# A two-layer streaming encoder step: activations, memory, states and vectors handed over as columns, weights by granules

## The chip, the cores and the metric

The kernel runs on one core of one Trainium2 chip. The metric is device time in microseconds, the median of three runs. Beside it there is one profiled execution with a trace, from which all views below come.

## The reference

One inference step of a two-layer encoder over a prompt of 512 tokens and a sample of 32 tokens that carries state. Each sub-layer is followed by a LayerNorm of `ALPHA * x + sublayer(x)`. All data is float32, model width 1024.

```python
def run_trunk(x, pos, mem_k, mem_v, states, ...):
    for layer in range(DEPTH):                       # DEPTH = 2
        x = post_norm(x, 0.5 * swiglu(x, ffn_up[layer, 0], ffn_down[layer, 0]), ...)
        if layer % 2 == 0:
            y, st = mixer_ab(x, pos, *states[layer], ...)   # RG-LRU beside chunked retention
        else:
            y, st = mixer_c(x, *states[layer], ...)         # RWKV-7 time mixing
        x = post_norm(x, y, ...)
        x = post_norm(x, cross_attn(x, mem_k[layer], mem_v[layer], xa_q[layer], xa_o[layer]), ...)
        x = post_norm(x, 0.5 * swiglu(x, ffn_up[layer, 1], ffn_down[layer, 1]), ...)
    return x, new_states

def reference(x_prompt, x_sample, mem_prompt, state_conv0, ..., cache_mem_k, cache_mem_v, ...):
    mem_k_p = jnp.einsum('bmd,lde->lbme', mem_prompt, xa_k)   # 256 memory rows, 4 heads of 256
    mem_v_p = jnp.einsum('bmd,lde->lbme', mem_prompt, xa_v)
    y_prompt, st_p = run_trunk(x_prompt, pos_p, mem_k_p, mem_v_p, zero_states, ...)
    y_sample, st_s = run_trunk(x_sample, pos_s, cache_mem_k[..], cache_mem_v[..], sample_states, ...)
    return (y_prompt, y_sample, mem_k_p, mem_v_p, *st_p, *st_s)
```

The feed-forward is `(silu(x @ gate) * (x @ up)) @ down` with an inner width of 2816. RWKV-7 keeps a 64x64 state in each of 16 heads.

## The kernel before

**Layout.** Activations lie as columns: the model width on partitions (8 blocks of 128), tokens along the row. The 544 tokens are two halves: A has tokens 0 to 255, B has 256 to 511 and the 32 of the sample (288 in all). Each half has x (tiles XA, XB) and x split in two parts that matmuls take exactly, high (XHA, XHB) and low (XLA, XLB); HH and HL hold the same for a sub-layer's inner result.

**Weights.** A weight matrix is cut in granules of 1024 (or 896) rows by 128 columns, 512 KB. A granule is loaded by SyncE (SP) to one of three raw buffers `wr`, split by ACT (high part, line 486) and by DVE or GpSimd (low part, lines 408 and 412) to one of five slots `W`, and used by `linear`: for each of 8 blocks the high and the low weights with the high x, then the high weights with the low x, 24 matmuls into a PSUM bank `mm`. Mostly A and B share a granule; in and around layer 1's mixer each half loads its own stream (`SOLO`), so that A can run ahead.

**Order.** Each part is a Python generator. A planner (`Clock`) gives every instruction a start by its own costs and due times and hands that to the scheduler as a priority; the order on each engine, and which of DVE and GpSimd takes a low part (`ett`), come out of that. Each engine and each DMA queue works strictly in its own order. So a change in one part may move instructions far away.

**What comes in and goes out as rows.** x, the memory, the cached keys, the parameter vectors and the small states arrive as rows of tokens or of 128 numbers and are turned to columns by transposes on TensorE (`K.tr`, line 400, against the identity `identt`), through the PSUM banks `ax` or `mm`, and read from there by ACT and DVE. `load_x` does it for x at the start, half A ahead of B; `store_x` turns the result back at the end, again through `ax`, with copies to `arena` and stores by SP. `mem_kv` computes the memory's keys and values for both layers, 32 granules threaded into the first feed-forward: each key block is stored as it is to the scratch `kt`, transposed, and stored to the output; each value block is transposed, and stored to the output and to the scratch `vt`. `attend` transposes the cached keys of the sample.

**RWKV in layer 1.** Chunks of 32 tokens run one after another (`wkv_chain`), the state in two tiles Y in turn (one is tile Q, the other a raw buffer wr). Beside the chain, `wkv_solve` solves a triangular system for each block of tokens by rows on GpSimd: multiplications into P and subtractions in LC (line 412), with the system fetched from the scratch `dn` and the result passed through the scratch `dz` to W. The last block is the sample's: it begins with the sample's state, loaded as rows and transposed. `state_out` transposes the final states of the prompt (after block 7) and of the sample (after block 8) and stores them by GpSimd's queue.

Of the kernel before, what the change touches and what calls it, by code (L numbers as in the profile page):

```python
# [22 lines left out]
NT = NA + NB  # L23
# [350 lines left out]
class Kern(Clock):  # L374
# [228 lines left out]
    def _load(self, s):  # L603

        k, g = s["next_raw"], s["g"]
        if k >= s["limit"] or len(s["raw"]) >= NRAW - 1 or len(self.raws.free) <= self.kept[1]:
            return None
        self.raws.free.sort(key=lambda t: t[:2])
        if self.raws.free[0][0] > self.now:
            return self.raws.free[0][0]  # L610
        r = self.raws.pop()
        ap, kc, m = g[k][:3]
        self.end = self.now
        self.dma(r[:, :kc, :m], ap.rearrange("(c p) m -> p c m", p=128))
        s["raw"][k] = (r, self.end)
        s["next_raw"] += 1
        return self.now
# [84 lines left out]
def load_params(K):  # L702
# [19 lines left out]
    two.append(("shift1", i["state_shift1"].rearrange("b j (r p) -> (b j r) p", p=128), 8))
    groups.append(two)
    tot = sum(n for g in groups for _, _, n in g)
    K.pv = K.pool.tile([128, tot], F32, name="pv")
    col = 0
    for g in groups:
        blk = yield from K.ar.take((128,))
        st, = blk
        r = 0  # L730
        for n, ap, k in g:
            K.dma(st[r:r + k], ap)
            VEC[n] = col + r
            r += k
        ps = yield from K.aux.take()
        K.tr(ps[:, :r], st[:r])
        K.vcopy(K.pv[:, col:col + r], ps[:, :r])
        K.aux.give(ps)
        blk.free()
        col += r  # L740
# [22 lines left out]
def program(K):  # L763
# [98 lines left out]
def half_main(K, h):  # L862
# [20 lines left out]
    yield from store_x(K, h)  # L883
# [11 lines left out]
def load_x(K, h):  # L895
# [5 lines left out]
    st = K.slot("HH" + h.name, [128, 8 * n])  # L901
    parts = [(K.i["x_prompt"][0, h.c0 + t * 128:h.c0 + t * 128 + 128], t * 128, 128, st[:, t * 1024:t * 1024 + 1024])
             for t in range(2)]
    if h is K.B:
        parts.append((K.i["x_sample"][0], 256, 32, K.slot("HLB", [128, 8 * n])[:, :1024]))
    for src, t0, m, st in parts:
        K.dma(st[:m], src)
    K.go = True
    yield
    for src, t0, m, st in parts:  # L910
        for q in range(2):
            ps = yield from K.aux.take()
            p3 = ps.rearrange("p (a b) -> p a b", a=4)
            for c in range(4):
# [5 lines left out]
            K.aux.give(ps)  # L920
            yield
    event(K, "x", h.name).fire(K)
    yield K.done()


def store_x(K, h):
    parts = [(K.o["y_prompt"][0, h.c0 + t * 128:h.c0 + t * 128 + 128], t * 128, 128) for t in range(2)]
    if h is K.B:
        parts.append((K.o["y_sample"][0], 256, 32))
    blks = []  # L930
    for dst, t0, m in parts:
        blk = yield from K.ar.take((1024,))
        blks.append(blk)
    for q in range(2):
        for (dst, t0, m), blk in zip(parts, blks):
            st = blk.aps[0][:m, q * 512:q * 512 + 512]
            ps = yield from K.aux.take()
            for c in range(4):
                K.tr(ps[:m, c * 128:c * 128 + 128], h.x[:, q * 4 + c, t0:t0 + m])
            (K.vcopy if t0 == 128 else K.act)(st, ps[:m])  # L940
            K.aux.give(ps)
            K.dma(dst[:, q * 512:q * 512 + 512], st)
    yield
    yield K.done()
    for blk in blks:
        blk.free()


def store_states(K):

    for e in ("tail", "h"):
        for j in range(4):
            yield event(K, e, "B", j)
    yield event(K, "shift", "B")
    blk = yield from K.ar.take((128,))
    st, = blk
    ps = yield from K.aux.take()
    K.tr(ps[:48, :128], K.ov)
    K.vcopy(st[:48], ps[:48, :128])
    K.aux.give(ps)  # L960
    o = K.o
    yield K.done()
    for nm, a, r in (("p_conv", 0, 12), ("s_conv", 12, 12)):
        K.dma(o[nm].rearrange("b j (r p) -> (b j r) p", p=128), st[a:a + r])
    for nm, a, r in (("p_lru", 24, 4), ("s_lru", 28, 4)):
        K.dma(o[nm].rearrange("b (r p) -> (b r) p", p=128), st[a:a + r])
    for nm, a, r in (("p_shift", 32, 8), ("s_shift", 40, 8)):
        K.dma(o[nm].rearrange("b j (r p) -> (b j r) p", p=128), st[a:a + r])
    yield K.done()
    blk.free()  # L970
# [97 lines left out]
def post_ln(K, h, l, e, whole=False, final=False):  # L1068
# [53 lines left out]
def mem_kv(K):  # L1122
# [10 lines left out]
    for l in range(2):  # L1133
        for ap in (i["xa_k"][l], i["xa_v"][l]):
            for j in range(8):
                gran.append(ap[:, j * 128:j * 128 + 128])
# [7 lines left out]
    for t in range(2):  # L1144
        K.dma(st, i["mem_prompt"][0, t * 128:t * 128 + 128])
        p3 = ps.rearrange("p (a b) -> p a b", a=4)
        for q in range(2):
            for c in range(4):
                K.tr(p3[:, c], st[:, (q * 4 + c) * 128:(q * 4 + c) * 128 + 128])
            hi, lo = mh[:, q * 4:q * 4 + 4, t * 128:t * 128 + 128], ml[:, q * 4:q * 4 + 4, t * 128:t * 128 + 128]  # L1150
            K.act(hi, p3)
            K.tt(lo, p3, hi.bitcast(F32), ALU.subtract)
# [4 lines left out]
    for g, ap in enumerate(gran):  # L1157
# [3 lines left out]
        dst = K.o["mem_v" if kind else "mem_k"][l, 0].rearrange("(t p) h d -> p t (h d)", p=128)  # L1161
        yield K.ready([raw])
        K.dma(raw, ap.rearrange("(c p) m -> p c m", p=128))
# [73 lines left out]
def attend(K, h, l, hd, q, hh, hl, c0, m, qe, fin):  # L1237
# [11 lines left out]
    else:  # L1249
        K.dma(r3[:, 0], K.i["cache_mem_k"][l, 0, :, hd].rearrange("(c p) d -> p c d", p=128))  # L1250
# [3 lines left out]
    if c0 == 0:  # L1254
        K.act(ks[:, 0], raw[:, 0])
        K.tt(ks[:, 1], raw[:, 0], ks[:, 0].bitcast(F32), ALU.subtract)
    else:
        ps = yield from K.aux.take()
        p3 = ps.rearrange("p (c n) -> p c n", c=2)
        for a in range(2):  # L1260
            for b in range(2):
                K.tr(p3[:, b, a * 128:a * 128 + 128], r3[:, 0, a, b * 128:b * 128 + 128])
        K.act(ks[:, 0], ps)
        K.tt(ks[:, 1], ps, ks[:, 0].bitcast(F32), ALU.subtract)
        K.aux.give(ps)
# [317 lines left out]
def setup_mix1(K):  # L1583
# [7 lines left out]
    K.dma(K.w2a2[0:64], i["l1_w2"])  # L1591
    K.dma(K.w2a2[64:128], i["l1_a2"])
# [9 lines left out]
def lora_weights(K, h):  # L1602
# [10 lines left out]
    for t, u, nm, p in ((g1, gm, "l1_g1", 5), (wa[:, :, 0:64], wm[:, :, 0:64], "l1_w1", 3),  # L1613
                        (wa[:, :, 64:128], wm[:, :, 64:128], "l1_a1", 4)):
        yield K.ready([t])
        K.dma(t, K.i[nm].rearrange("(c p) m -> p c m", p=128))
# [319 lines left out]
def state_out(K, w, Y, dst):  # L1936
    blk = yield from K.ar.take((16, 64))
    st, = blk
    for q in range(2):
        ps = yield from w.pl.take()  # L1940
        for g in range(8):
            K.tr(ps[0:64, g * 64:g * 64 + 64], Y[0:64, 8 * q + g])
        K.act(st[0:64, 8 * q:8 * q + 8], ps[0:64].rearrange("p (g k) -> p g k", g=8))
        w.pl.give(ps)
# [137 lines left out]
```

## Time and profile before

| What | Value |
|---|---|
| median of three runs | 2989.22 us (2982.29 to 2990.96) |
| the profiled execution's own time | 2981.34 us |
| its span in the profile | 2979.5 us |
| mean granted TensorE clock | 0.952 |
| instructions on PE / DVE / ACT / GpSimd | 22456 / 3094 / 2182 / 1201 |
| bytes read from and written to HBM | 313.09 MB, 13.92 MB |
| packets of the SP queue | 603328, for 310.93 MB |

A row of the trace has the time from the span's start, how long the instructions took, engine, line, operation and `out<-in` by tile names without buffer numbers; in brackets the idle time of the engine just before and what ended it. PE is TensorE's matmuls, PEld its weight loads, POOL is GpSimd, SPq SyncE's issue of DMAs. The chain is the work that ended last, followed back from the end.

### The profile page before, as it was taken

The numbers are of one execution on the slowest core, as the hardware profiler recorded it, in microseconds if no ns is written. First come the engines' busy times: TensorE is split into PE (matmuls) and PEld (weight loads), VectorE is DVE, ScalarE is ACT, GpSimd is POOL, SyncE is SP. The second block draws the span as 40 slices with busy tenths as digits, with TensorE's granted clock in tenths as the row PEclk, the third lists the DMA queues.
The fourth block names the chain that finished last, engine by engine and source line by source line (L and its number), as shares of the span: only waits on it lengthen the run. The fifth ranks groups of instructions, "written<-read, shape, count | busy, mean of one in ns | idle before, by whom it ended". The sixth has DMA issues, their size and how long they took to land.

```text
span 2979.5 us, 54689 instructions
## 1 busy us (share of the span) xinstructions
PE 2809.6 (94%) x22456; PEld 2701.7 (91%) x22456; DVE 1765.9 (59%) x3094; ACT 1276.8 (43%) x2182; POOL 909.1 (31%) x1201
## 2 busy tenths in 40 slices
PE   8999998999998999998999899799779989999998
PEld 8999998898898999998999899578678878999997
DVE  5333436677767333356345655877588657765665
ACT  4323233665555222234234443444345454654444
POOL 2000104433314000023001212588577764241311
PEclk9999999999999999999999999799678889999999
DMA  6443443223232332322346554133122245546563
GB/s 184 124 120 116 134 117 107 77 75 90 89 98 71 100 89 82 93 79 85 86 138 184 143 145 128 38 90 98 42 70 80 75 115 167 149 144 181 167 174 94
DMA packets 611035, 330.56 MB, mean 111 GB/s; under 512 B 29032, under 2 KB 603840, under 8 KB 610784
## 3 DMA queue, kind: packets, MB, share of 16 engines
q1 hardware_dynamic: 603328, 310.93, 36.3%
q0 software_dynamic: 7456, 16.13, 2.0%
q8 instruction: 176, 2.88, 0.4%
q14 instruction: 75, 0.61, 0.1%
HBM read 313.09 MB, written 13.92 MB: 110 GB/s over the span
## 4 chain that ended last, share of the span: by engine, by line
PE 71%; DVE 11%; POOL 7%; ACT 5%; issue 3%; DMA 3%; SPq 0%; DVEq 0%; ACTq 0%; POOLq 0%
PE mm L395 65%; PE ax L395 5%; POOL LC L412 2%; POOL P L412 2%; DVE W L408 2%; ACT arena L486 2%; DVE arena L408 1%; DVE arena L432 1%; ACT W L486 1%; PE ax L400 1%; DVE XA L408 1%; DMA wr<-in_ffn_up 1%; POOL arena L412 1%; ACT L2043 1%; DVE XB L408 1%
## 5 line engine op out<-in xcount | busy, mean ns | idle before, releaser
L486 ACT ACTIVATE W<-wr 128x1024 fp32r<-128x1024 f32 (+1 forms) x558 | 577.7, 1038 | 725.8 <-PE mm L395 587.1
L408 DVE TENSOR_TENSOR W<-wr,W 128x1024 fp32r<-128x1024 f32 (+1 forms) x453 | 562.4, 1244 | 541.2 <-ACT W L486 536.8
L395 PE MATMUL mm<-XHB,W 128*128 128x288 f32 x3840 | 581.0, 300 | 15.4 <-ACT XHB L486 4.8
L395 PEld LDWEIGHTS mm<-XHB,W 128*128 128x128 f32 x3840 | 528.3, 190 | 24.1 <-ACT XHB L486 5.8
L395 PE MATMUL mm<-XHA,W 128*128 128x256 f32 x3840 | 530.8, 288 | 16.4 <-ACT XHA L486 6.6
L395 PEld LDWEIGHTS mm<-XHA,W 128*128 128x128 f32 x3840 | 494.8, 193 | 25.9 <-ACT XHA L486 10.8
L412 POOL TENSOR_TENSOR W<-wr,W 128x1024 fp32r<-128x1024 f32 (+1 forms) x105 | 253.9, 2419 | 659.7 <-ACT W L486 652.7
L395 PE MATMUL mm<-XLB,W 128*128 128x288 f32 x1984 | 313.6, 298 | 1.4 <-DVE XLB L408 1.4
L395 PE MATMUL mm<-HHB,W 128*128 128x288 f32 x1920 | 291.6, 302 | 9.7 <-ACT W L486 3.5
L395 PE MATMUL mm<-XLA,W 128*128 128x256 f32 x1984 | 290.5, 285 | 2.3 <-POOL XLA L412 2.3
L395 PE MATMUL mm<-HHA,W 128*128 128x256 f32 x1920 | 271.7, 290 | 14.5 <-DVE XA L408 5.0
L395 PEld LDWEIGHTS mm<-XLB,W 128*128 128x128 f32 x1984 | 281.2, 190 | 3.4 <-DVE XLB L408 1.9
L395 PEld LDWEIGHTS mm<-HHB,W 128*128 128x128 f32 x1920 | 268.7, 192 | 12.8 <-ACT W L486 4.5
L395 PEld LDWEIGHTS mm<-HHA,W 128*128 128x128 f32 x1920 | 250.7, 194 | 20.5 <-ACT W L486 5.3
L395 PEld LDWEIGHTS mm<-XLA,W 128*128 128x128 f32 x1984 | 261.6, 191 | 4.5 <-POOL XLA L412 2.5
L486 ACT ACTIVATE arena<-mm 128x256 f32<-128x256 f32 (+4 forms) x292 | 112.6, 388 | 308.2 <-PE mm L395 289.9
L432 DVE SCALAR_TENSOR_TENSOR arena<-mm,arena 128x288 f32<-128x288 f32 (+1 forms) x176 | 77.3, 439 | 161.7 <-PE mm L395 143.7
L395 PE MATMUL mm<-HLB,W 128*128 128x288 f32 x896 | 142.7, 299 | 0.0
L395 PE MATMUL mm<-HLA,W 128*128 128x256 f32 x896 | 129.9, 284 | 0.0
L412 POOL TENSOR_TENSOR SUMA<-XA 128x256 f32<-128x256 f32 x16 | 14.4, 901 | 377.3 <-DVE XA L408 360.7
L395 PEld LDWEIGHTS mm<-HLB,W 128*128 128x128 f32 x896 | 129.3, 192 | 0.1
L412 POOL TENSOR_TENSOR LC<-LC,P 128x66 f32<-128x66 f32 (+24 forms) x279 | 122.7, 440 | 20.6
(430 smaller groups left out, 3769.6 us busy)
## 6 DMA issues: line engine op xcount, KB each, us to landing
wr<-in_ffn_up SPq DMA_DIRECT2D x246, 512.0 KB
wr<-in_ffn_down SPq DMA_DIRECT2D x96, 448.0 KB
wr<-in_l_w_rkv SPq DMA_DIRECT2D x48, 512.0 KB
wr<-in_ffn_down SPq DMA_DIRECT2D x40, 512.0 KB
wr<-in_l_w_in SPq DMA_DIRECT2D x24, 512.0 KB
wr<-in_l_w_out SPq DMA_DIRECT2D x24, 512.0 KB
wr<-in_xa_q SPq DMA_DIRECT2D x24, 512.0 KB
wr<-in_xa_o SPq DMA_DIRECT2D x24, 512.0 KB
```

The lines of the kernel that those rows point to most:

```text
L395: self.nc.tensor.matmul(out, lhsT, rhs, start=start, stop=stop)
L400: self.nc.tensor.transpose(out, in_, self.ident[k0:k0 + k, k0:k0 + k])
L408: self.nc.vector.tensor_tensor(out, a, b, op=op)
L412: self.nc.gpsimd.tensor_tensor(out, a, b, op=op)
L432: self.nc.vector.scalar_tensor_tensor(out, a, s, b, op0=op0, op1=op1)
L486: return self.nc.scalar.activation(out, a, f, bias=bias, scale=scale, **kw)
L2043: nc.scalar.preload_act_table_set(name)
```

## The change

The host now hands the inputs over in the layouts in which the kernel keeps them (`lay`), and takes the outputs as columns (`unlay`). On the chip this removes the transposes of x, the memory, the cached keys, the vectors, the RWKV states and the outputs, and their reads from PSUM. Weights lie in HBM granule by granule, each as 128 rows of 4 KB (3.5 KB for 896 rows) in the place of 1024 pieces of 512 B. The values of the memory keep their transposes, since attention reads them as rows.

```diff
 _load:
-        self.dma(r[:, :kc, :m], ap.rearrange("(c p) m -> p c m", p=128))
+        self.dma(r[:, :kc, :m], ap)
 load_params (three groups of vectors, 20 loads and 3 transposes, become one load):
+    K.pv = K.pool.tile([128, i["pv"].shape[1]], F32, name="pv")
+    K.dma(K.pv, i["pv"])
 program:
-            gran.append((ap[k0:k1, m:m + 128], (k1 - k0) // 128, 128))
+            gran.append((ap[m // 128, :, k0 // 128:k1 // 128], (k1 - k0) // 128, 128))
 load_x:
-    for src, t0, m, st in parts:
-        K.dma(st[:m], src)
+    for c in range(0, 8, 2):
+        (K.dma, K.adma)[c // 2 % 2 if h is K.A else 0](h.x[:, c:c + 2], K.i["x"][:, c:c + 2, h.c0:h.c0 + n])
...
-                K.tr(p3[:, c, :m], st[:m, (q * 4 + c) * 128:(q * 4 + c) * 128 + 128])
-            d = (slice(None), slice(q * 4, q * 4 + 4), slice(t0, t0 + m))
-            K.act(h.xh[d], p3[:, :, :m])
-            K.tt(h.xl[d], p3[:, :, :m], h.xh[d].bitcast(F32), ALU.subtract)
-            K.vcopy(h.x[d], p3[:, :, :m])
+    for c in range(0, 8, 2):
+        u = slice(c, c + 2)
+        K.act(h.xh[:, u], h.x[:, u])
+        K.tt(h.xl[:, u], h.x[:, u], h.xh[:, u].bitcast(F32), ALU.subtract)
 store_x is gone; post_ln, last LayerNorm:
             first(c)
             second(c)
+            if final:
+                K.dma(K.o["y"][:, c, h.c0:h.c0 + n], x[:, c])
 store_states (a transpose and six stores become one store):
+    K.dma(K.o["ov"], K.ov)
 mem_kv:
+        K.gdma(K.o["mem_v" if kind else "mem_k"][l, j * 128:j * 128 + 128], a)
         if kind == 0:
             K.gdma(K.kt[l][j * 128:j * 128 + 128], a)
+            yield K.done()
+            continue
...
-        K.gdma(dst[:, :, j * 128:j * 128 + 128], b)
-        if kind:
-            K.gdma(K.vt[l].rearrange("(t p) d -> p t d", p=128)[:, :, j * 128:j * 128 + 128], b)
+        K.gdma(K.vt[l].rearrange("(t p) d -> p t d", p=128)[:, :, j * 128:j * 128 + 128], b)
 attend (sample half):
-        K.dma(r3[:, 0], K.i["cache_mem_k"][l, 0, :, hd].rearrange("(c p) d -> p c d", p=128))
+        K.dma(r3[:, 0], K.i["cache_k"][l, hd])
...
-                K.tr(p3[:, b, a * 128:a * 128 + 128], r3[:, 0, a, b * 128:b * 128 + 128])
-        K.act(ks[:, 0], ps)
+    K.act(ks[:, 0], raw[:, 0])
 wkv_chain (the sample's block, and the two final states):
-            K.dma(st[0:64], K.i["state_wkv1"][0].rearrange("h v k -> v h k"))
-            yield K.done()
-            for q in range(2):
-                for g in range(8):
-                    K.tr(b1[0:64, g * 64:g * 64 + 64], st[0:64, 8 * q + g])
-                K.act(Y[0:64, 8 * q:8 * q + 8], b1[0:64].rearrange("p (g k) -> p g k", g=8))
+            yield K.ready([Y[0:64]])
+            K.dma(Y[0:64], K.i["wkv0"])
...
-                yield from state_out(K, w, Yn, K.o["p_wkv"][0])
+                K.gdma(K.o["p_wkv"], Yn[0:64])
```

What this does to the order, at three places.

TensorE at the start. XHA, XLA and XHB are the parts of x, HHA and HHB hold its rows before, `mm` and `ax` are PSUM banks. Before:

```order
L400 MATMUL ax_67<-identt,HHA_93 128x128 x4
L395 MATMUL mm_63<-XHA_91,W_1_71 128x256
L400 MATMUL ax_68<-identt,HHB_101 128x128 x4
L400 MATMUL ax_69<-identt,HHB_101 128x128 x4
L395 MATMUL mm_64<-XHA_91,W_2_72 128x256
L395 MATMUL mm_63<-XHA_91,W_1_71 128x256 x15
L395 MATMUL mm_63<-XLA_92,W_1_71 128x256 x8
```

And now, from PE's first instruction on:

```order
L395 MATMUL mm_63<-XHA_91,W_1_71 128x256 x16
L395 MATMUL mm_63<-XLA_92,W_1_71 128x256 x8
L395 MATMUL mm_64<-XHA_91,W_2_72 128x256 x16
L395 MATMUL mm_64<-XLA_92,W_2_72 128x256 x8
L395 MATMUL mm_65<-XHB_100,W_1_71 128x288 x16
```

Half A's first two weight blocks no longer have the transposes of half B's rows among them; half B comes in third.

ACT at the end, from the LayerNorm of half B's last sub-layer on. Before, with the reads of the transposed result from `ax`:

```order
L486 ACTIVATE arena_79<-ax_70 128x288
L486 ACTIVATE arena_79<-arena_79,epst 128x288
L486 ACTIVATE arena_79<-arena_79 128x288
L486 ACTIVATE XB_98<-XB_98,pv,lng_345 128x288 x8
L486 ACTIVATE arena_79<-ax_69 128x512
L486 ACTIVATE arena_79<-ax_68 32x512
L486 ACTIVATE arena_79<-ax_67 128x512
L486 ACTIVATE arena_79<-ax_69 32x512
```

And now:

```order
L486 ACTIVATE arena_79<-XB_99 128x288 x8
L486 ACTIVATE arena_79<-ax_68 128x288
L486 ACTIVATE arena_79<-arena_79,epst 128x288
L486 ACTIVATE arena_79<-arena_79 128x288
L486 ACTIVATE XB_99<-XB_99,pv,lng_195 128x288 x8
```

The normalised columns are the engine's last work; SP's last rows are the eight stores of them.

GpSimd at the end of the last solve. P and LC are the solve's tiles, `dz` the scratch through which its result goes. Before:

```order
L412 TENSOR_TENSOR P_115_17677<-LC_7380,P_115_17677 128x16
L412 TENSOR_TENSOR LC_7380<-LC_7380,P_115_17677 128x8x2
L491 DMA out_p_wkv<-arena_80 64x16x64
L412 TENSOR_TENSOR P_115_17677<-LC_7380,P_115_17677 128x8
L412 TENSOR_TENSOR LC_7380<-LC_7380,P_115_17677 128x8
L491 DMA dz_17682<-LC_7380 128x1x32
```

And now:

```order
L412 TENSOR_TENSOR LC_7233<-LC_7233,P_112_17512 128x7x7
L412 TENSOR_TENSOR P_112_17512<-LC_7233,P_112_17512 128x42
L491 DMA out_p_wkv<-Q_113_17514 64x1024
L412 TENSOR_TENSOR LC_7233<-LC_7233,P_112_17512 128x7x6
L412 TENSOR_TENSOR P_112_17512<-LC_7233,P_112_17512 128x35
```

The store of the prompt's state stands ahead of the solve's last eleven instructions instead of its last two, and it goes directly from tile Q, into which SP then loads the sample's state (`in_wkv`); behind that load SP has weight loads of half A.

More of the change, by code (lines that the diff above doesn't have):

```diff
@@ L954, in store_states @@
     yield event(K, "shift", "B")
[L955 to L970, printed above, removed]
+    K.dma(K.o["ov"], K.ov)
 def ffn(K, h, l, e):
@@ L1143, in mem_kv @@
     st, = blk
[L1144 to L1152, printed above, removed]
+    for q in range(2):
+        u = slice(4 * q, 4 * q + 4)
+        s4 = st.rearrange("p (c t) -> p c t", c=4)
+        K.dma(s4, i["mem"][:, u])
+        K.act(mh[:, u], s4)
+        K.tt(ml[:, u], s4, mh[:, u].bitcast(F32), ALU.subtract)
         yield K.done()
@@ L1253, in attend @@
     ks = yield from K.keys.take()
[L1254 to L1261, printed above, removed]
-                K.tr(p3[:, b, a * 128:a * 128 + 128], r3[:, 0, a, b * 128:b * 128 + 128])
-        K.act(ks[:, 0], ps)
-        K.tt(ks[:, 1], ps, ks[:, 0].bitcast(F32), ALU.subtract)
-        K.aux.give(ps)
+    K.act(ks[:, 0], raw[:, 0])
+    K.tt(ks[:, 1], raw[:, 0], ks[:, 0].bitcast(F32), ALU.subtract)
     t = K.done()
@@ L1933, in wkv_load @@
         event(K, "load", ci).fire(K)
[L1936 to L1940, printed above, removed]
-        for g in range(8):
-            K.tr(ps[0:64, g * 64:g * 64 + 64], Y[0:64, 8 * q + g])
-        K.act(st[0:64, 8 * q:8 * q + 8], ps[0:64].rearrange("p (g k) -> p g k", g=8))
-        w.pl.give(ps)
-    K.gdma(dst.rearrange("h v k -> v h k"), st[0:64])
-    yield K.done()
-    blk.free()
 def wkv_chain(K, w):
@@ L1959, in wkv_chain @@
         if L == 32:
-            blk = yield from K.ar.take((16, 64))
-            st, = blk
-            yield K.ready([st])
-            K.dma(st[0:64], K.i["state_wkv1"][0].rearrange("h v k -> v h k"))
-            yield K.done()
-            for q in range(2):
-                for g in range(8):
-                    K.tr(b1[0:64, g * 64:g * 64 + 64], st[0:64, 8 * q + g])
-                K.act(Y[0:64, 8 * q:8 * q + 8], b1[0:64].rearrange("p (g k) -> p g k", g=8))
-            blk.free()
+            yield K.ready([Y[0:64]])
+            K.dma(Y[0:64], K.i["wkv0"])
         yield event(K, "load", ci)
@@ new lines, with lay, cols @@
+SHORT = {"state_lru0": "lru0", "state_conv0": "conv0", "state_shift1": "shift1", "ln_g": "ln_g", "ln_b": "ln_b"}
+OUTS = [("y", (128, 8, NT)), ("mem_k", (2, 1024, 256)), ("mem_v", (2, 1024, 256)), ("ov", (128, 48)),
+        ("p_ret", (1, 4, 128, 128)), ("p_wkv", (64, 16, 64)), ("s_ret", (1, 4, 128, 128)), ("s_wkv", (64, 16, 64))]
+def lay(inputs):
+    g = {k: np.asarray(v) for k, v in inputs.items()}
+    out = {}
+    def cols(a):
+        return a.T.reshape(8, 128, -1).transpose(1, 0, 2)
+    out["x"] = cols(np.concatenate([g["x_prompt"][0], g["x_sample"][0]]))
+    out["mem"] = cols(g["mem_prompt"][0])
+    for n in ("ffn_up", "ffn_down", "xa_q", "xa_k", "xa_v", "xa_o", "l0_w_in", "l0_w_out", "l1_w_rkv", "l1_w_out"):
+        a = g[n]
+        k, m = a.shape[-2:]
+        a = a.reshape(a.shape[:-2] + (k // 128, 128, m // 128, 128))
+        d = a.ndim - 4
+        out[n] = a.transpose(tuple(range(d)) + (d + 2, d + 1, d, d + 3))
+    rows = []
+    at = 0
+    for n in VECS:
+        r = g[n].reshape(-1, 128)
+        VEC[SHORT.get(n, n[3:])] = at
+        at += len(r)
+        rows.append(r)
+    pv = np.concatenate(rows).T
+    out["pv"] = pv
+    out["l1_wa1"] = cols(np.concatenate([g["l1_w1"], g["l1_a1"]], 1).T)
+    out["l1_g1"] = cols(g["l1_g1"].T)
+    out["l1_wa2"] = np.concatenate([g["l1_w2"], g["l1_a2"]])
+    out["l1_g2"] = g["l1_g2"]
+    out["cache_k"] = g["cache_mem_k"][:, 0].transpose(0, 2, 3, 1).reshape(2, 4, 2, 128, 256).transpose(0, 1, 3, 2, 4)
+    out["cache_mem_v"] = g["cache_mem_v"]
+    out["wkv0"] = g["state_wkv1"][0].transpose(2, 0, 1)
+    for n in ("state_ret0", "l0_lru_wa", "l0_lru_wx"):
+        out[n] = g[n]
+    return out
@@ new lines, in unlay @@
+def unlay(o):
+    y = o["y"].transpose(1, 0, 2).reshape(1024, NT).T
+    ov = o["ov"].T
+    mem = [o[n].transpose(0, 2, 1).reshape(2, 1, 256, 4, 256) for n in ("mem_k", "mem_v")]
+    st = []
+    for p in range(2):
+        st.append((ov[12 * p:12 * p + 12].reshape(1, 3, 512), ov[24 + 4 * p:28 + 4 * p].reshape(1, 512),
+                   o["sp"[1 - p] + "_ret"], ov[32 + 8 * p:40 + 8 * p].reshape(1, 1, 1024),
+                   o["sp"[1 - p] + "_wkv"].transpose(1, 2, 0)[None]))
+    return (y[None, :512], y[None, 512:], *mem, *st[0], *st[1])
```

95 lines of the change are left out of this document (14 added, 81 removed), and 3 rows, old and new, of the table INS.

## The prediction

> **What bounds the kernel now.** I read the busy table first, then the chain that ended last, then the stretches, then the chain in time. The columns of the first fence: engine, busy us, share of the span, instructions; then the chain's shares by engine and by line.
>
> ```profile
> PE 2809.6 (94%) x22456; PEld 2701.7 (91%) x22456; DVE 1765.9 (59%) x3094; ACT 1276.8 (43%) x2182; POOL 909.1 (31%) x1201
> PE 71%; DVE 11%; POOL 7%; ACT 5%; issue 3%; DMA 3%; SPq 0%; DVEq 0%; ACTq 0%; POOLq 0%
> ```
>
> TensorE is the bound over the kernel, but the chain leaves it for 29% of the span. So a transpose removed counts in full where PE never pauses, and elsewhere only if what PE waits for comes earlier too. The stretches say where that is (from:to, length, busy us and count of PE, PEld, DVE, ACT, POOL, then granted clock, DMA share, GB/s):
>
> ```profile
> 0.00:73.00 73.00, 65.31 (x495) 64.02 (x496) 39.47 (x89) 33.08 (x51) 16.29 (x12) 0.98 0.65 188
> 73.00:485.00 412.00, 412.00 (x3304) 411.95 (x3303) 160.48 (x224) 120.44 (x183) 44.93 (x62) 1.00 0.42 122
> 485.00:940.00 455.00, 420.15 (x3169) 405.65 (x3168) 332.18 (x854) 248.90 (x510) 169.32 (x169) 0.96 0.30 88
> 940.00:1665.00 725.00, 716.80 (x5646) 713.23 (x5646) 328.83 (x486) 244.89 (x383) 78.03 (x51) 0.99 0.36 102
> 1665.00:2610.00 945.00, 845.61 (x7183) 762.56 (x7182) 670.39 (x1137) 458.93 (x809) 514.57 (x854) 0.88 0.36 102
> 2610.00:2979.00 369.00, 349.71 (x2669) 344.34 (x2667) 234.59 (x308) 170.55 (x249) 85.99 (x55) 0.99 0.53 152
> ```
>
> From 73 to 485 us (first feed-forward, with the memory keys and values threaded in) PE has no gap at all. The 99 us of PE idle in 1665 to 2610 (945.00 - 845.61) belong to layer 1's mixer and its edges. The chain in the solid stretch gives the two prices that I use throughout:
>
> ```profile
> 72.68 0.22 PE mm L400 x2
> 72.90 14.99 PE mm L395 x120
> 87.89 0.22 PE mm L400 x2
> ```
>
> A weight matmul costs 14.99/120 = 0.125 us, and a 128x128 transpose 0.11 us, on the path.
>
> **The change, term by term**, against the profiled execution (2981.34 us, span 2979.5). The order loses 212 transposes on PE, 27 instructions on DVE, 15 on ACT.
>
> *Start.* PE's first rows, and the two splits of the first weight granule:
>
> ```profile
> 5.21 2.79 PE L400 MATMUL ax<-identt,HHA 128*128 128x128 f32 x12 [5.21 <-DMA HHA<-in_x_prompt]
> 8.53 1.05 ACT L486 ACTIVATE W<-wr 128x1024 fp32r<-128x1024 f32 x1
> 10.56 1.22 DVE L408 TENSOR_TENSOR W<-wr,W 128x1024 fp32r<-128x1024 f32 x1
> 11.32 1.10 PE L400 MATMUL ax<-identt,HHB 128*128 128x128 f32 x8 [1.30 <-DMA HHB<-in_x_prompt]
> 12.17 3.59 PE L395 MATMUL mm<-XHA,W 128*128 128x256 f32 x16
> 12.38:15.79 3.41, 3.41 (x19) 3.41 (x18) 2.99 (x5) 1.33 (x3) 1.64 (x1) 0.50 1.14 302
> ```
>
> In the first 73 us PE runs 495 instructions, of which 61 are transposes (40 of x, 18 of memory, 3 of vectors). The other 434 are worth 434 x 0.125 = 54.2 us, so 18.8 us go to the start. Half A waits in order behind half B's transposes, and those wait for B's rows. Afterwards PE's first instruction is a weight matmul. As many bytes stand ahead of the first granule as now, so it has landed by 8.53; with the two splits the second matmul can start at 8.53 + 1.05 + 1.22 = 10.8. ACT was busy with x until about then, and A's four loads of x now come over two queues, two of them issued by ACT ahead of its table load, so I take 10.3. Against that, x comes in pieces of 1 KB instead of 4: if those move no better than 512 B does (296 GB/s against 407, rows below), its 1 MB takes up to 1 us longer. One window at half clock (last row, 0.50) stays: 3.41/2 = 1.7. The start then loses 12.0 and saves 6.8; small stalls on later granules bring me to **6.0**. Bounds: 2 (starting at 12.17 as now, with two half-clock windows, the transposes alone gone) and 8.5 (no half-clock window). What hides the new splits of x from SBUF, eight each on ACT and DVE, is the wait for the first granule; A's four stand ahead of its split, so if x lands late they delay it by about 0.6 each.
>
> *Transposes where PE is solid.* The key half of the memory work loses two per granule, 32 in all, 2 of them already in the start: 30 x 0.11 = **3.3**. The next rows (ns: least, median, most; first and last start) are half A's 16 output transposes, and the stretch of layer 0's attention that holds 16 of the 32 for the cached keys:
>
> ```profile
> L400 PE MATMUL ax<-identt,XA x16: 270/272/330, 2852.5 to 2855.5; 128*128 128x128 f32 x16
> L400 PE MATMUL ax<-identt,arena x56: 220/272/328, 804.3 to 897.3; 128*128 128x128 f32 x48, 32*128 32x32 f32 x8
> ```
>
> A's output takes 3.3 us from first to end and 16 x 0.11 = 1.8 of pure work while half B has matmuls ready: **1.8** (0 to 3.3). Of the cached keys' 32 x 0.11 = 3.5 I count half, **1.7** (0 to 3.5), since both attentions pause for softmax. These come to 6.8. The PSUM reads on ACT and DVE that go with them I cost at nothing: matmuls cover those, and if PE ran dry there they would be worth about 0.6 each (the 0.59 of the store's read below).
>
> *Weight loads.* Each 512 KB granule was 1024 pieces of 512 B and is now 128 of 4096 B, the shape in which x's rows already arrive. First row: x's rows alone in flight; second: weights alone.
>
> ```profile
> 3.50:5.25 1.75, 0.04 (x1) 0.07 (x2) 0.00 (x0) 0.00 (x0) 0.00 (x0) 1.00 1.02 407
> 1729.50:1730.75 1.25, 1.25 (x13) 1.25 (x12) 0.00 (x0) 0.66 (x2) 0.00 (x0) 1.00 1.02 296
> ```
>
> At the same full share the engines move 407 GB/s against 296: 512 KB in 1.29 us instead of 1.77, 0.48 less a load. That counts only where a load is on the chain, which is 13 times, eleven of them in the stretch with the 99 us of gaps. Here are the first, three that follow one another as layer 1 begins, and the last:
>
> ```profile
> 600.15 5.17 DMA wr<-in_l_w_in
> ...
> 1735.72 5.11 DMA wr<-in_ffn_up
> 1744.83 5.48 DMA wr<-in_ffn_up
> 1753.89 4.74 DMA wr<-in_ffn_up
> ...
> 2665.94 4.73 DMA wr<-in_ffn_up
> ```
>
> 13 x 0.48 = **6.3**. Bounds: 0, if the split of the granule (1.05 on ACT, 1.22 on DVE) or the free buffer is late next; and 10.4, by 0.8 a load, the difference between two 128 KB stores in pieces of 1024 and 512 B:
>
> ```profile
> kt<-arena POOLq DMA_DIRECT2D x16, 128.0 KB, 2.1
> out_mem_k<-arena POOLq DMA_DIRECT2D x16, 128.0 KB, 2.9
> ```
>
> [...]
>
> *End.* Columns as in the start; the last row is SyncE's issue of the last store.
>
> ```profile
> 2969.18 4.64 ACT L486 ACTIVATE XB<-XB,pv,lng 128x288 f32<-128x288 f32 x8 [2.00 <-DVE XB L408]
> 2969.86 5.66 PE L400 MATMUL ax<-identt,XB 128*128 128x128 f32 x24 [5.80 <-ACT XB L486]
> 2975.56 0.59 ACT L486 ACTIVATE arena<-ax 32x512 f32<-32x512 f32 x1 [0.24 <-PE ax L400]
> 2976.28 0.41 SPq L491 DMA_DIRECT2D out_y_sample<-arena  x1
> ```
>
> Half B's normalised columns are ready at 2969.18 + 4.64 = 2973.82, and the last store is issued at 2976.28. Afterwards each column's store follows its own ACT instruction, so the last goes out 2.4 earlier; it is 144 KB instead of 64, some 0.2 longer at 407 GB/s. **2.2** (1 to 2.9). Eight issues at about 0.4 on SP keep pace with columns every 4.64/8 = 0.58.
>
> *Layer 1's states.* 48 small transposes and six reads on ACT go, but a hand-over is new: the prompt's final state is stored straight from the tile Q, and the sample's state is loaded into the same tile, so SP's load waits for POOL's store to land, with weight loads behind it on SP.
>
> ```profile
> 2405.72 0.65 SPq L491 DMA_DIRECT2D arena<-in_state_wkv  x1
> 2407.30 0.33 POOL L412 TENSOR_TENSOR P<-LC,P 128x42 f32<-128x42 f32 x1
> 2411.61 0.87 POOL L491 DMA_DIRECT2D out_p_wkv<-arena  x1 [0.53 <-issue]
> 2418.78 1.67 POOL L491 DMA_DIRECT2D W<-dz  x3 [2.66 <-DMA dz<-LC]
> DMA to landing us min/median/max: 3.6/3.6/3.6
> ```
>
> The store's new place on POOL is behind the row of 2407.30, so it is out at 2407.6, lands by 2411.2 (3.6, last row, that of out_p_wkv), and the load, taken to be as long, at 2414.8. The chunk needs the solved block too, which POOL only fetches from 2418.78 on: hidden. SP is held until 2411.2 instead of 2405.72; the weight loads behind it go 5.5 later, against 48 transposes less. I take **+0.7** saved, between 4 saved and 8 lost.
>
> *The rest.* Fewer vector loads on SP, one store for the small states, LoRA weights in one load: nothing, under the solid stretch (412.00 of 412.00 busy) or the 725 us one.
>
> Sum: 6.0 + 6.8 + 6.3 + 2.2 + 0.7 = 22.0 saved, 2981.3 to 2959.3 for the profiled execution. That execution lies 7.9 below the median of the three runs, 2989.2; against the median the forecast is **2967**. The likeliest case's own range is 2957 to 2976.
>
> **Rivals.** *Loads give nothing*: what a load gains, the split behind it or the next free buffer takes back; 22.0 - 6.3 = 15.7 saved, 2973.5. For it: a load is issued only once DVE has split the buffer's last granule, as 1735.72, 1744.83 and 1753.89 follow one another at 9 us. Against: of those 9 about 5 are the load itself. [...]
>
> *More comes back*: the upper ends, 8.5 + (3.3 + 3.3 + 3.5) + 10.4 + 2.9 + 4 = 35.9, and where three loads run one after another the freed buffer brings the next load forward too, which the chain's 13 do not count; 2953, down to 2944 if loads off the chain give 10 more. For it: the 13 loads take about 5 us each where 1.77 is transfer.
>
> *Gone into layer 1*: the early terms stand, but the planner hands out layer 1's work anew and its waits grow by what is won, 14 us or more: within 9 of no change, about 2984. Against: PE's order differs little outside layer 0's mixer.
>
> *Slower*: the solves of layer 1 run on POOL in order, and any weight split set among them holds them up:
>
> ```profile
> L412 POOL TENSOR_TENSOR LC<-LC,P 128x66 f32<-128x66 f32 (+24 forms) x279 | 122.7, 440 | 20.6
> L412 POOL TENSOR_TENSOR W<-wr,W 128x1024 fp32r<-128x1024 f32 x14 | 33.8, 2413 | 13.2 <-ACT W L486 13.2
> ```
>
> A split there costs 2.41. Ten more among the nine solves cancel the gain, and 13 or more make the kernel slower by over 9 us (22.0 + 9 = 31 = 13 x 2.41), 2998 or more. Against: counted in the order there are five now and four afterwards; only waits could do it.
>
> **How the numbers follow.** The forecast's case has 0.50, loads nothing 0.18, more comes back 0.17, gone into layer 1 0.10, slower 0.05. Below 0.3% (9 us) this kernel's time cannot be told from no change; so faster 0.85, same 0.10, slower 0.05. The range runs from the far end of "more" to the near part of "gone": 2944 to 2982.
>
> **What would show it.** Start: PE's first weight matmul near 10 and the solid stretch reached some 6 us earlier. Transposes: no PE L400 pairs in the chain before the value granules. Loads: chain rows of about 4.5 instead of 5, and DMA share down at the same bytes. End: no PE after the last statistics. States: in_wkv issued on SP within 4 us of out_p_wkv, and no PE gap behind it. It is wrong if PE idle between 1665 and 2610 grows past 99 us, or if the first granule lands after 10.

## The result, and the profile after

The changed kernel takes 2949.9 us (median; 2942.2 to 2954.2), before 2988.2: the ratio is 0.987, 95% interval 0.9852 to 0.9889. It is faster by 38 us, where 22 were forecast (2967, range 2944 to 2982). The two profiled executions lie 27.1 apart, 2981.3 and 2954.2: that of before was 6.9 under the median of its kernel, that of the changed kernel 4.3 over its own. A second trace of the changed kernel (run e0 below) took 2948.9.

The busy table and the chain's shares of the changed kernel, in the columns of the prediction's first fence:

```profile
PE 2787.8 (94%) x22244; PEld 2683.9 (91%) x22244; DVE 1770.2 (60%) x3067; ACT 1270.3 (43%) x2165; POOL 871.0 (29%) x1190
...
PE 76%; DVE 11%; POOL 6%; ACT 3%; issue 3%; DMA 1%; SPq 0%; DVEq 0%; ACTq 0%; POOLq 0%
```

PE is busy for 21.8 us less, and DMA's share of the chain fell from 3% to 1%. The stretches of the changed kernel, cut at the places that answer to those of before:

```profile
0.00:62.00 62.00, 52.25 (x393) 51.96 (x394) 33.10 (x71) 30.86 (x44) 9.95 (x10) 1.00 0.65 213
62.00:474.00 412.00, 412.00 (x3314) 411.95 (x3313) 161.96 (x202) 122.35 (x187) 59.84 (x70) 1.00 0.40 122
474.00:924.00 450.00, 421.90 (x3167) 406.30 (x3165) 332.63 (x868) 251.90 (x512) 156.60 (x163) 0.97 0.30 91
924.00:1648.50 724.50, 716.27 (x5635) 713.01 (x5634) 325.96 (x476) 241.43 (x379) 78.82 (x53) 0.99 0.34 102
1648.50:2585.00 936.50, 840.55 (x7133) 758.69 (x7132) 687.77 (x1147) 456.71 (x804) 489.38 (x844) 0.88 0.35 103
2585.00:2952.40 367.40, 344.85 (x2615) 341.95 (x2613) 228.76 (x306) 167.07 (x243) 76.37 (x51) 0.97 0.51 153
```

PE's idle time in layer 1's mixer and its edges is 96.0 us (936.50 - 840.55), against 99.4 before. The start runs at full clock now (1.00).

A span can be split in three: PE's idle time (span less busy), what PE loses at half clock (estimated as half of its busy time in the trace's stretches at 0.50), and its work at full clock (the rest):

| us | span | PE idle | lost at half clock | work at full clock |
|---|---|---|---|---|
| before | 2979.5 | 169.9 | 110.8 | 2698.8 |
| changed | 2952.4 | 164.6 | 110.1 | 2677.7 |
| changed, second trace | 2947.1 | 163.9 | 107.8 | 2675.4 |

21.1 and 23.4 of the 27.1 and 32.4 us are work that PE no longer has; 212 transposes by the prediction's 0.11 make 23.3. Waits and clock give the other 6 to 9. The rest of the 38 us is how single executions lie to their medians; no trace shows where a usual execution of the kernel before spends it.

The next table says where. In every kernel the time is taken at the same weight matmul by count (of 17,280, number 11,041, where layer 1's mixer begins, and number 15,361 in the last feed-forward); all but the first row and the last two columns are differences to before. These are single traces; those of "memory" and "keys" are the slowest executions of their kernels.

| kernel | up to layer 1 | layer 1 | after | idle there | lost at half clock there |
|---|---|---|---|---|---|
| before | 1657.0 | 1047.9 | 274.7 | 104.6 | 90.7 |
| changed | -16.5 | -10.6 | 0.0 | 99.8 | 88.9 |
| changed again (e0) | -17.6 | -13.9 | -0.9 | 99.7 | 87.1 |
| granules alone (e1) | +1.3 | -2.2 | 0.0 | 103.3 | 91.0 |
| changed, rows again (e2) | -15.6 | -7.9 | -1.0 | 102.0 | 90.1 |
| other tile (e3) | -18.7 | -27.9 | -0.9 | 90.1 | 81.2 |
| other tile, columns on two (e4) | -17.1 | -20.4 | -4.6 | 93.6 | 86.9 |
| x alone (e5) | -5.9 | +8.8 | +3.1 | 94.4 | 109.1 |
| memory alone (e6) | -6.1 | +24.4 | +1.5 | 95.8 | 117.5 |
| keys alone (e7) | +1.1 | +13.7 | +1.2 | 110.4 | 102.4 |
| states alone (e8) | +4.7 | -5.6 | +3.6 | 107.0 | 87.7 |
| output alone (e9) | -0.2 | +2.4 | -1.4 | 106.4 | 91.2 |

Where two kernels run the same instructions in the same order on every engine, the table shows how far single traces scatter. Up to layer 1 that holds for e8 and before (4.7 apart). Up to half A's output it holds for e9 and before (2.4 in layer 1), and for e3 and e4 (7.5 in layer 1). So a difference of a few us in one cell proves little by itself.

### The profile page after: what moved, and what is told of

It reads as the page before. It is cut to its first block, busy times and chain, and to the rows that moved or that the text cites. A ratio compares the mean times of both kernels' runs of the same rounds, so it can differ in the third digit from the quotient of the medians.

```text
span 2952.4 us, 54187 instructions
## 1 busy us (share of the span) xinstructions
PE 2787.8 (94%) x22244; PEld 2683.9 (91%) x22244; DVE 1770.2 (60%) x3067; ACT 1270.3 (43%) x2165; POOL 871.0 (29%) x1190
## 4 chain that ended last, share of the span: by engine, by line
PE 76%; DVE 11%; POOL 6%; ACT 3%; issue 3%; DMA 1%; SPq 0%; DVEq 0%; ACTq 0%; POOLq 0%
PE mm L395 70%; PE ax L395 4%; POOL LC L412 2%; POOL P L412 2%; DVE arena L408 2%; DVE W L408 1%; DVE arena L432 1%; ACT arena L486 1%; DVE XB L408 1%; DVE XA L408 1%; DVE XLA L408 1%; PE ax L400 1%; ACT W L486 1%; ACT XHA L486 1%; DVE Q L408 1%
## 5 line engine op out<-in xcount | busy, mean ns | idle before, releaser
L408 DVE TENSOR_TENSOR W<-wr,W 128x1024 fp32r<-128x1024 f32 (+1 forms) x461 | 571.4, 1241 | 537.6 <-ACT W L486 536.1
L412 POOL TENSOR_TENSOR W<-wr,W 128x1024 fp32r<-128x1024 f32 (+1 forms) x97 | 236.4, 2437 | 679.7 <-ACT W L486 621.4
L395 PEld LDWEIGHTS mm<-HHB,W 128*128 128x128 f32 x1920 | 267.8, 190 | 15.7 <-DVE W L408 5.3
L486 ACT ACTIVATE arena<-mm 128x256 f32<-128x256 f32 (+3 forms) x292 | 112.7, 388 | 297.4 <-PE mm L395 282.5
L412 POOL TENSOR_TENSOR LC<-LC,P 128x66 f32<-128x66 f32 (+24 forms) x279 | 115.9, 415 | 20.2
```

The costliest lines, as they stand in the source:

```text
L395: self.nc.tensor.matmul(out, lhsT, rhs, start=start, stop=stop)
L408: self.nc.vector.tensor_tensor(out, a, b, op=op)
L412: self.nc.gpsimd.tensor_tensor(out, a, b, op=op)
L486: return self.nc.scalar.activation(out, a, f, bias=bias, scale=scale, **kw)
```

## The experiments

**The loads, in both directions.** e1 is the kernel before with the weights in granules, e2 the changed kernel with its weights in rows. Every engine's order stays as it was in each.

```diff
 _load (e1; e2 the other way round; the memory's weights likewise)
-        self.dma(r[:, :kc, :m], ap.rearrange("(c p) m -> p c m", p=128))
+        self.dma(r[:, :kc, :m], ap)
```

> The kernel before with one change: every weight granule stored as 128 pieces of 4096 B, so that a load is 128 pieces instead of 1024. No instruction is added, removed or moved on any engine. Theory A (a load on the chain gets shorter, as in the prediction's term): 13 loads on the chain of before; by the landings of the changed kernel's trace a load lands about 0.2 us earlier, by the prediction's term 0.48: 2.6 to 6.3 us faster than before, 2982 to 2986. Theory B (loads give nothing, the split or the free buffer is late next): within 1 us of before. Theory C (three loads in a row bring each other forward): 10 us or more faster, 2978 or less. The chain's rows of weight loads fall from 13 only in A and C.

> The changed kernel with its weights back in rows of 512 B pieces, all else as changed and in the same order on every engine. Theory A: 2.6 to 6.3 us slower than the changed kernel, 2953 to 2956. Theory B: the same as the changed kernel, 2950, so that the whole gain of 38 is from the columns. Theory C: 10 us or more slower, 2960 or above.

> The changed kernel once more, for the spread: runs so far 2942.2 to 2954.2. If the profiled run was an outlier of its kernel, the median stays near 2950 and a second trace shows the same places with smaller pauses; every pause that both traces show is of the kernel and not of the run.

Measured: e1 2980.6 against 2988.9 (ratio 0.9981, 0.9969 to 0.9994: 1.8 to 9.3 us faster); e2 2956.6 against e0's 2950.1. So the granules are worth 6.5 in the changed kernel and 8.3 by medians (5.7 by the ratio) in the kernel before: theory A, at its upper end. From 2988.9 to 2956.6 the columns give the other 32. The tile view of `in_ffn_up` shows how, first e2, then e0 (ns of an issue: least, median, most; the second row is what ScalarE's splits waited for these loads, in us, and how often):

```profile
L491 SPq DMA_DIRECT2D wr<-in_ffn_up x246: 367/368/1129, 2.2 to 2891.8; - x123
...
  ACT W L486: 72.0, 41
...
DMA to landing us min/median/max: 3.6/4.0/7.6
```

```profile
L491 SPq DMA_DIRECT2D wr<-in_ffn_up x246: 327/328/745, 2.2 to 2883.9; - x123
...
  ACT W L486: 42.0, 30
...
DMA to landing us min/median/max: 3.2/3.6/8.5
```

A load lands 0.4 earlier. Between e2 and e0 the chain's loads of weights fall from 13 to 3, these of e0:

```profile
2.18 6.01 DMA wr<-in_ffn_up
...
2416.28 4.36 DMA wr<-in_ffn_up
...
2640.41 4.24 DMA wr<-in_ffn_up
```

Between before and e1 they fall from 13 to 6. The number on the chain is that of one execution in one order: kernels with rows have 6 (e5) to 13 there, kernels with granules 3 to 7. That ten loads fewer are worth 6 us and not 50 fits with the work that is late next taking a load's place; this is inferred, not shown.

**The state's hand-over.** Forecast as hidden, it stands on the changed kernel's chain; the middle fence is of PE, the last of VectorE, which writes the prompt's final state:

```profile
2381.60 2.92 DMA out_p_wkv<-Q
2384.65 3.61 DMA Q<-in_wkv
```

```profile
2388.40 1.08 PE L395 MATMUL ax<-Q,W 96*32 96x64 f32 x32 [5.81 <-DMA Q<-in_wkv]
```

```profile
2376.10 1.48 DVE L408 TENSOR_TENSOR Q<-Q,pc 64x512 f32<-64x512 f32 x2
```

The state is complete at 2376.10 + 1.48 = 2377.6, its store leaves POOL only at 2381.60, behind the solve's steps in POOL's order, and the sample's load must wait until it has landed (at 2384.52; the load leaves at 2384.65). In the kernel before, PE waited at this place only for the state itself (the next line), and in e0 it waits longer than in the changed kernel's first trace (the line below it):

```profile
2400.50 1.06 PE L400 MATMUL ax<-identt,Q 64*64 64x64 f32 x8 [3.75 <-DVE Q L408]
```

```profile
2386.06 1.08 PE L395 MATMUL ax<-Q,W 96*32 96x64 f32 x32 [8.16 <-DMA Q<-in_wkv]
```

e3 loads the sample's state into the other state tile:

```diff
 wkv_chain (and the same in wkv_load, which waits for chunk e - 2)
-        Y, Yn, TB = w.y[ci % 2], w.y[(ci + 1) % 2], w.tb[b % 2]
+        e = ci + (L == 32)
+        Y, Yn, TB = w.y[e % 2], w.y[(e + 1) % 2], w.tb[b % 2]
```

> The changed kernel, in which the sample's state is loaded into the other of the two state tiles, so that the load no longer waits until the store of the prompt's state has landed, but for the last matmuls that read that tile. If the hand-over costs what the chain shows (store 2.92 us, then load 3.61 us, PE idle 5.81 us): PE's pause there falls by the store's 2.9 us to about 3, and the kernel is 2 to 4 us faster, 2946 to 2948. Rival: the planner's order behind it changes, and the time moves by some us either way for other reasons, which the pause at that place alone tells apart. If the pause stays at 5 us or more, the store was not what held the load.

Measured: 2934.4 (2932.2 to 2942.9), ratio to before 0.9825 (0.9808 to 0.9841), clear of the changed kernel's 0.9873 (0.9858 to 0.9887). It beats both kernels, by 15.7 us against e0 where 2 to 4 were expected. In e3 the load leaves at 2365.41, 4.5 us ahead of the store, which POOL issues at 2369.9 (the chain, then PE):

```profile
2365.41 3.50 DMA wr<-in_wkv
```

```profile
2369.04 0.65 PE L395 MATMUL ax<-wr,W 96*32 96x64 f32 x16 [2.24 <-DMA wr<-in_wkv]
```

The pause at this place was 8.16 in e0's trace and is 2.24 now. The expectation took only the store's landing; POOL's queue ahead of the store (2377.6 to 2381.60) was as large.

Not all of the 15.7 is the tile's. Up to the hand-over both kernels run the same instructions in the same order on every engine, and at PE's first instruction whose order differs e3's trace is already 4.4 earlier than e0's (2353.3 against 2357.7), by less half clock. From there to weight matmul 15,361 it takes 305.0 us, against 317.5 and 315.6 in the two traces of the changed kernel; e4, in the same order as e3, takes 310.5. PE's idle time there is 16.4 in e3 and 18.8 in e4, against 22.6 and 26.4; the loss at half clock (5.4 and 10.4 against 12.7 and 6.0) does not tell them apart. So by these traces the other tile is worth 5.1 to 12.5 us. The planner's order after this place is new too, and what that adds was not told apart.

**Each part of the columns alone**, on the kernel before, by the diff of the change:

> The kernel before with the first part of the change alone: x arrives as columns, the vectors as one block already in columns. The question of this and the next runs of one part each is where 32 us come from: the columns of all parts together took 32 (2988.9 to 2956.6), the prediction's terms for them give 15.7. Prediction's term for the start: 6.0 faster, 2983. By the changed kernel's trace the start gains 7.4. Rival (a later pause goes with it: the 7.1 us in which PE stood idle behind the first feed-forward, in the changed kernel 2 to 3): 10 to 13 faster, 2976 to 2979, and that pause is short in this trace too.

> The kernel before with the memory's part alone: the memory arrives as columns, its keys and values leave as columns, 48 transposes fewer (16 of the memory, 32 of the keys). Prediction's terms: 3.3 for the keys, and 16 x 0.11 = 1.8 of the start's transposes: 5.1 faster, 2984. Rival (it is the lighter ACT and DVE during the first feed-forward that shorten the pause of 7.1 us behind it): 9 to 11 faster, 2978 to 2980.

> The kernel before with the cached keys alone in columns: 32 transposes of 0.11 us fewer in the two attentions. Prediction's term: 1.7 faster, 2987, bounds 0 and 3.5. Rival (the planner sets the work of the later stages anew): 3 us or more either way.

> The kernel before with layer 1's states alone handed over without transposes: 48 small transposes and six reads on ACT fewer, but the sample's state is loaded into the tile from which the prompt's state is being stored. Prediction: 0.7 faster, between 4 faster and 8 slower. Theory from the trace of the changed kernel (the hand-over stands on the chain, 5.8 us of PE pause and a stretch at half clock behind it): 2 to 8 slower, 2991 to 2997, with a pause of PE over 4 us ahead of the sample's chunk. Rival (the hand-over hidden, the removed work pays): up to 4 faster, and no pause.

> The kernel before with the output alone in columns: 68 transposes and their reads fewer, each column stored as it is ready. Prediction's terms: 2.2 at the end and 1.8 for half A: 4.0 faster, 2985. By the trace of the changed kernel the end gives 2.5 and half A's output loses 2 (PE waits 3.6 us there behind ACT's eight final columns and a table load): 0.5 faster, 2988.

Measured by medians against before in the same job: x +1.5 (ratio 1.0003, 0.9992 to 1.0014), memory +7.4 (1.0017, 1.0000 to 1.0034), keys +7.5 (1.0022, 1.0010 to 1.0034), states -2.7 (0.9983, 0.9971 to 0.9995), output -2.2 (0.9992, 0.9981 to 1.0003). The parts alone add up to +11.5 (by the ratios to +5, give or take 9), together they give -32. For x and memory no expectation held as a time, for the keys the rival's did. The output's -2.2 lies between its two expectations, and the interval holds both. Its transposes are 40, not 68: 616 of 656 are left in e9's trace.

Yet each part does its own work. Memory alone has the end of the first feed-forward 5.7 earlier (5.1 expected). The pause of 7.1 us behind that feed-forward is gone with x alone and stays with memory alone (first before, then the longest pause left there in e5, then e6, then the changed kernel):

```profile
519.53 0.58 PE L395 MATMUL mm<-VA,W 128*128 128x256 f32 x1 [7.09 <-DVE arena L443]
```

```profile
508.51 0.44 PE L400 MATMUL mm<-identt,arena 128*128 128x128 f32 x2 [1.76 <-ACT arena L486]
```

```profile
513.82 0.58 PE L395 MATMUL mm<-VA,W 128*128 128x256 f32 x1 [7.09 <-DVE arena L443]
```

```profile
504.17 0.49 PE L395 MATMUL mm<-VA,W 128*128 128x256 f32 x1 [0.72 <-DVE arena L443]
```

In before and in e6 the copy that frees a memory granule's bank stands behind VectorE's eight subtractions of the layer norm for each half; in e5 and in the changed kernel it comes ahead of half B's. Both x and memory alone reach layer 1 about 6 us early, and lose it there. Here are layer 1's mixer in before and in e6, cut at the same weight matmuls:

```profile
1657.00:2557.10 900.10, 800.71 (x6812) 718.34 (x6812) 639.90 (x1074) 424.01 (x744) 508.85 (x851) 0.87 0.36 99
```

```profile
1650.90:2575.70 924.80, 832.83 (x6813) 741.51 (x6812) 637.96 (x1073) 423.55 (x744) 500.04 (x851) 0.85 0.35 97
```

As many matmuls take 32 us longer, at less idle time (92.0 against 99.4) and a granted clock of 0.85 instead of 0.87. The loss at half clock is 25 of the 32. The other executions of e6 show it too, the trace being the slowest of ten: the mean clock of a run is 0.947 in the median against 0.951 of before. In a span of 2985 us 0.004 of mean clock is 24 us at half clock instead of full, by estimate up to 12 us of time. That x and memory alone came out slow goes with the clock (medians 0.9485 and 0.947); for the keys (0.950) it allows about 3 of the 7.5 us, and their trace has 5.8 more idle time in layer 1. Why these orders get a lower clock is not shown.

States alone keep the hand-over's pause and are still faster:

```profile
2414.65 1.08 PE L395 MATMUL ax<-Q,W 96*32 96x64 f32 x32 [6.83 <-DMA Q<-in_wkv]
```

In the kernel before PE paused 3.75 at this place, ahead of the state's transposes. The removed transposes pay more than the longer pause costs: the rival of that expectation in the time, its theory in the pause.

**The order anew, with no part changed.** The planner's fixed cost of a transfer goes from 60 to 70, in the kernel before (e10) and in the changed one (e11):

```diff
-        self.plan("dma", n / 350 + 60, [out], [a], queue)
+        self.plan("dma", n / 350 + 70, [out], [a], queue)
```

> The kernel before with one number of the planner changed: the fixed cost that it assumes for a transfer, 60 to 70. The same instructions run on every engine, in another order from layer 0's mixer on. Theory O (what single parts lost, 5 to 7 us each, and part of what all together won, is the new order that every edit brings: PE's idle time and the stretches at half clock in layer 1's mixer come out otherwise): the time moves by 4 to 20 us either way, and the whole move lies between the first feed-forward and the last one. Rival P (the parts themselves cost it): within 3 us of before, 2984 to 2990.

> The changed kernel with the same number of the planner changed, 60 to 70. Theory O: 4 to 20 us away from 2950; if the order of the changed kernel was lucky, slower, 2954 to 2970. Against the kernel before with this number, the change then gives the prediction's 22 and a remainder of either sign, where the pair at 60 gave 38. Rival P: 2947 to 2953, and a difference of 38 between the two again.

Measured: e10 2984.9 against 2988.7 (ratio 0.9993, 0.9973 to 1.0013), e11 2948.4. Between the two lie 36.5 us, between the pair at 60 lay 38. So theory O falls for these two orders: the gain of all parts together does not hang on one order. But the eleven runs of e10, one kernel in one order, reach from 2973.8 at a mean clock of 0.954 to 3005.0 at 0.945. So an unchanged kernel moves by 31 us from run to run, and its clock with it, nearly as far as the whole change; this limits what a single trace can tell.

**Half A's output.** PE pauses 3.61 there in the changed kernel, where the stretch from 2825 to 2885 of before held 2.1 us of idle time in all. ScalarE finishes eight columns and loads a table before it reads the bank that PE needs. First ScalarE, then PE, in the changed kernel:

```profile
2817.58 4.03 ACT L486 ACTIVATE XA<-XA,pv,lng 128x256 f32<-128x256 f32 x8
2821.63 1.28 ACT L1929 ACT_TABLE_LOAD   x1
2822.92 0.41 ACT L486 ACTIVATE arena<-mm 128x288 f32<-128x288 f32 x1
```

```profile
2818.55 1.23 PE L395 MATMUL mm<-XLB,W 128*128 128x288 f32 x8
2823.39 4.21 PE L395 MATMUL mm<-XHB,W 128*128 128x288 f32 x16 [3.61 <-ACT arena L486]
```

And the same place in the kernel before, again ScalarE first:

```profile
2855.32 1.28 ACT L2043 ACT_TABLE_LOAD   x1
2856.62 0.41 ACT L486 ACTIVATE arena<-mm 128x288 f32<-128x288 f32 x1
```

```profile
2852.46 1.25 PE L400 MATMUL ax<-identt,XA 128*128 128x128 f32 x10
2854.38 1.42 PE L400 MATMUL ax<-identt,XA 128*128 128x128 f32 x6 [0.66 <-ACT XA L486]
2857.08 2.38 PE L395 MATMUL mm<-XHB,W 128*128 128x288 f32 x16 [1.28 <-ACT arena L486]
```

So half B's matmuls waited for the same read before. The 16 transposes ran inside that wait; without them the wait is hardly shorter, PE stands idle in it, and the granted clock drops (0.50 over the next 16 matmuls, 1.00 over those of before). Output alone (e9) brings the pause too, 3.16 us.

e4 is e3 with every second column of the final layer norm on VectorE:

```diff
-        if c % 2 and not final:
+        if c % 2:
```

> The kernel of the other state tile, and in the final layer norm every second column is finished by VectorE instead of all eight by ScalarE, as in the other layer norms. If ScalarE's order (eight columns of 0.50, then a table load of 1.28, then the read that frees PE's bank) makes PE wait 3.6 us at half A's output: that pause falls below 2 us and the end comes 1 to 2 us earlier, 2929 to 2932 against 2934. Rival (VectorE, with two operations for each column already, is the later one there): no change or 1 to 2 us slower.

```profile
2816.60 2.37 PE L395 MATMUL mm<-XHB,W 128*128 128x288 f32 x16 [1.12 <-ACT arena L486]
```

The pause fell to 1.12 as expected, but the time is 2939.4 (2934.9 to 2940.3) against e3's 2934.4. From the last weight matmul to the end e4 takes 18.1 us where e3 takes 17.1: at half B's end VectorE is the later one, the rival's loss of 1. Yet from weight matmul 15,361 on, where alone the two orders differ, e4's trace is 3.7 faster in sum (270.1 against 273.8). It is 9 slower ahead of that, where every engine runs the same in both: spread. So the edit seems to gain there, but the time of the whole is inconclusive; only half A should have it.

## Why the prediction was right or wrong, point by point

- **Start (6.0)**: right, a little small. PE's first weight matmul is at 9.07 (near 10 was forecast), the window at half clock is gone. The end of the first feed-forward is 10.7 and 11.4 earlier in the two traces (at number 3,800 of the matmuls that are not transposes); less the memory's 3.3 that makes 7.4 to 8.1, within 2 to 8.5. In the single parts it is 6.5 (4.1 for x and 5.7 for the memory there, less 3.3).
- **Memory's transposes (3.3)**: right. Alone, with the two steps at the start, 5.7 against 48 x 0.11 = 5.3.
- **Cached keys (1.7)**: not borne out. Alone they are 7.5 slower, with more idle time and more half clock in layer 1 by that trace. In the whole change their part cannot be told apart.
- **Loads (6.3)**: right, by both directions (5.7 to 8.3 and 6.5); 0.4 a load was measured for 0.48 (4.0 us to landing in pieces of 512 B in e2, 3.6 in granules in e0). The other factor, 13 loads on the chain, was luck in part: e5, with the same loads in rows, has 6. The rival that they give nothing falls.
- **Half A's output (1.8)**: wrong in sign. From weight matmul 15,361 to the last one the two traces are 1.6 and 2.4 slower. The step that failed is "while half B has matmuls ready": they were not ready, the bank was still to be read by ScalarE, and the transposes had filled that wait. Now it is a pause of 3.6, and the next 16 matmuls took 4.21 us where they take 2.29 at full clock. With the read earlier (e4) the same stretch is 2.8 faster than before.
- **End (2.2)**: right; from the last weight matmul to the end 20.0 us before, 17.5 after.
- **Layer 1's states (+0.7)**: the failed step is "hidden". The argument was that the chunk needs the solved block, which comes later. Its first product, state by keys, needs no solved block, and nothing else stood ahead of it in PE's order. The store's late turn on POOL, its landing and the load all stood in that step, and all were taken as hidden. SP's load followed the store by 3 us, within the 4 forecast, but the pause behind it was 5.8 and not none. The sign held all the same: e8 is 2.7 faster, and PE's work at full clock in layer 1 falls by 4.9 (852.5 to 847.6) with the 48 small transposes. That measure is rough: kernels with the same transposes there as before have 851.4 (e1) to 859.0 (e6).
- **Layer 1 as a whole** (the table's column, with its attention): 0.7 of states, 0.9 for half of the cached keys and twelve loads by 0.48 make 7.3; the traces show 10.6 and 13.9. The loads have 2.7 and 6.0 of them (from e2's 7.9), where 5.8 were forecast. The columns have 7.9 instead of 1.5: 4.6 of PE's work at full clock (852.5 to 847.9), 2.6 of idle time, 0.6 of half clock. The step that failed is the opening one: a transpose counts in full only where PE never pauses. In layer 1, with 100 us of idle time, the removed work came back too, because the idle time did not grow in its place; by single traces, and with the scatter named above, this is likely and not proven.
- **What no term had**: the pause behind the first feed-forward, 12.4 us of idle time to 7.8 around it, and the clock. The "wrong if" conditions (idle above 99 us, first granule after 10) did not occur.

So the time lay 17 below the forecast. Some 11 of them are where the two profiled executions lie in their kernels' spread (6.9 and 4.3): the prediction set its sum against the median as it stood, and the median of before is 1 lower this time. The other 5 are of the sum: up to layer 1 the traces show 6 more than its terms (16.5 against 10.6: the start, the keys of the memory, half the cached keys and one load), mostly the pause; in layer 1 some 3 more (10.6 against 7.3); behind it 4 less (0.0 against 4.0), mostly half A's output.

The range held, but the likeliest case's own (2957 to 2976) did not: 2949.9 lies where the rival "more comes back" had put the time (2953, down to 2944). That rival's reason did not come true: the loads gave 6 to 8 and not 10.4 or more, and half A's output lost about 2 instead of giving 3.3. So the sum had 22 of the 38 us, and it came as near to the traces' 27 as it did because misses of either sign cancelled.

## What to carry to other kernels

Work taken from the bounding engine can pay in stages where it idles as well, and can pay nothing where it only fills a wait; ask whether the waits there depend on that work. When a store and a load share a tile, price the whole way: the store's turn in its queue, its landing and the load (4.0, 2.92 and 3.61 us here); a second tile takes the first two away (in e3 the load left 4.5 us ahead of the store). And test single parts in the whole, as e2 did, not only alone: five parts of this change measured alone add up to no gain, together they give 32 us; why they lose so much alone stays open.

## What the runs showed of the hardware

The clock is a term of the sum. By the estimate above PE loses 102 (e3) to 138 us (e6) of a run to half clock, with nearly the same instructions. At half A's output the longer pauses cost more than themselves: 16 matmuls that take 2.29 us at a granted clock of 1.00 took 4.21 at 0.50 in the changed kernel after a pause of 3.61 (3.31 in e0), 4.21 after one of 3.15 in e3, and 2.37 after one of 1.12 in e4. In e0 this stretch of 27 us stayed at half clock with PE busy for 18 of them:

```profile
1853.71:1881.02 27.31, 18.13 (x127) 12.82 (x128) 24.57 (x52) 8.24 (x15) 8.05 (x7) 0.51 0.17 57
```

In the traces of before and of the changed kernel the stretches at half clock last 3.41 to 37.55 us, each of them one to eleven times 3.41 (but for the last of each trace, which the end cuts off); in the longest (before, from 2108.16 on) PE was busy for 28.66 us. What starts and ends them is not shown. Equal runs differ by clock (0.945 to 0.954 and 31 us in e10); no run shows the cause of that either.
